# The spatial part of a gated mixing, made for the prompt's four tiles at once instead of two and two

## The chip, the cores and the metric

The kernel runs on one core of one Trainium2 chip. The metric is the device time of one execution in microseconds, the median of several runs. The core has a matmul engine (TensorE, "PE" in the profile; its weight loads are "PEld"), VectorE ("DVE"), ScalarE ("ACT"), GpSimdE ("POOL") and SyncE ("SP"), which issues the DMA transfers here.

## The reference

One step of a small streaming encoder with two layers, in fp32. A prompt of 512 frames (four tiles of 128 rows) and a sample batch of 8 x 16 frames (one tile) go through the same layers; the sample also reads caches of 1,024 frames. Each layer projects its input once and feeds three branches: a chunked gated mixing (A), a latent attention (B) and a stick-breaking attention (C). Their results are normalised, joined and projected, and a squared-ReLU MLP follows. The change is in branch A:

```python
def spatial_gate(u, v, w_s, b_s):
    b, s = u.shape[:2]
    c = min(s, GMLP_CHUNK)            # 128
    n_c = s // c
    idx = jnp.arange(c)
    w = jnp.where(chunk_visible(idx, idx)[None], w_s[:, :c, :c], 0)
    vc = v.reshape(b, n_c, c, G_A, DG_A)
    mixed = jnp.einsum('gij,bnjgd->bnigd', w, vc) + b_s[:, :c].T[None, None, :, :, None]
    return u * mixed.reshape(b, s, G_A, DG_A)
...
    u = jax.nn.gelu(a_u).reshape(b, s, G_A, DG_A)
    v = layer_norm(jax.nn.gelu(a_v).reshape(b, s, G_A, DG_A))
    y_a = spatial_gate(u, v, w_s, b_s).reshape(b, s, W_A)
...
    y = jnp.concatenate([rms_norm(y_a, g_a), rms_norm(y_b, g_b), rms_norm(y_c, g_c)], -1)
```

G_A is 4 groups of DG_A = 64 columns. A tile of 128 frames is one chunk, so each of the prompt's tiles is mixed by the same four 128 x 128 matrices.

## The kernel before, in words

Every fp32 matrix is split into a high and a low fp32r part (`split`: a ScalarE copy, then a VectorE difference), and a product is three matmuls (`mm3`, line 634). Two streams run beside each other: P (the prompt, and the projections of all five tiles) and S (the sample). A layer of P goes through the stages in, mix, mla, out and mlp; S goes through prep, smla, ssb, out and mlp, and begins its layer when the mix of that layer has been emitted.

The mix stage (`p_layer`) has two lanes: the prompt's stick-breaking attention (`lane_psb`) and `rest`. `rest` projects u and v, and then runs two lanes against each other (`lanes`, line 468; the one with the smaller matmul time divided by its weight goes next, if its operands are ready): `latents` with weight 1.0 and `gmlp` with weight 0.1 (`WM`, line 42). `latents` makes two projections, five tiles each: 384 columns (evicted by `rms_to` into `ev`, stored to `cqd`) and then 320 columns (`latent_to`: an rms norm and a rotation with two little tiles, stored to `ckd`). `gmlp` applies the gelu and calls `gm_weights` and `gm_group` for the sample tile, and then for the prompt's tiles 1 and 2, and 3 and 4. A group normalises `gv` (the v half), splits it into `gh`, multiplies by the split mixing weights `wsT`, adds the bias `bsc`, multiplies by `u` and normalises each tile into `xy` with `rms_to`.

The order of the work is made by a planner in the file. The emission is recorded as a list of operations; `ranks` (line 193) gives each a priority by its place in its stream, and `schedule` (line 209) plays all engines with a cost for each operation and lays down the order of every engine, DMA issues on SP included. Three things in it bind the order further. The slots of a ring (a tag with a number of buffers) are granted in the order of emission, and a tile's first instruction does not come before that of the tile emitted before it on the same ring (`grant`, line 271, and `begun`, line 250). The matmul results of the projections lie in `acc`, a ring of three PSUM banks; those of the mixing in `sC`, another ring of three. And the little sums and roots of `rms_to` (line 678) come from rings of three in stream P (line 541). A tile may begin only when all tiles of closed pools that lie under it in SBUF are done (`under`, line 241): pools grow from the left and from the right end, and `spans` gives their places.

At the mix stage the left stack holds, from byte 85,760: `xT` (32,768 bytes per partition), `xS` 8,192, `gcq` 1,536, `gckv` 1,024, `rope` 2,560, `ev` 4,096, `gvt` 5,120, `gmxa` 1,024, `gt` 2 x 2,048, `wsT` 4,096, `bsc` 32, `gh` 4,096, and two rope tiles of 256; it ends at 154,912. The sample's preparation (`s_prep`) lies on the right and reaches down to 155,360: `kd` from there, `qd` from 155,872, `wuT` from 159,968 to 168,160. `wuT` is made from a staging buffer of a ring of three, and the first cache loads of smla (`rawK`) lie on that ring's bytes.

```python
    def little(shape, dtype, tag):
        return sm.tile(shape, dtype, tag=tag + now["by"], name=tag, bufs=3 if now["by"] == "P" else 2)
    def rms_to(out, src, g, n):
        ss = little([128, 1], F32, "ss")
        act.activation(junk[now["by"]][:, :n], src, AF.Square, accum_out=ss)
        r = rstd_of(ss, 1.0 / n, 1)
        dve.scalar_tensor_tensor(out, src, r[:, 0:1], g, ALU.mult, ALU.mult)
```

Of the kernel before, what the change touches and what calls it, by code (L numbers as in the profile page):

```python
# [11 lines left out]
F32 = mybir.dt.float32  # L12
F32R = mybir.dt.float32r
BF16 = mybir.dt.bfloat16
AF = mybir.ActivationFunctionType
ALU = mybir.AluOpType
# [34 lines left out]
def r32(ap):  # L51
    return ap.bitcast(F32)


class Pace:
# [37 lines left out]
    def ready(self, *xs):  # L93
        return max([self.done.get(x.tensor.name, 0.0) for x in xs])
# [420 lines left out]
def hybrid_step(  # L515
# [11 lines left out]
    act, dve, pool, pe = (Timed(e, k, pace) for e, k in ((nc.scalar, "act"), (nc.vector, "dve"), (nc.gpsimd, "pool"), (nc.tensor, "pe")))  # L527
# [13 lines left out]
    def little(shape, dtype, tag):  # L541
        return sm.tile(shape, dtype, tag=tag + now["by"], name=tag, bufs=3 if now["by"] == "P" else 2)
# [38 lines left out]
    def bank(tag):  # L581
        return ps.tile([128, 512], F32, tag=tag, name=tag, bufs=BUFS[tag])

    def at(tag, *xs):

        return max([pace.bank((id(ps), tag), BUFS[tag])] + [x if isinstance(x, float) else ready(x) for x in xs])
# [43 lines left out]
    def split(hi, lo, src, lo_eng=None):  # L630
        act.copy(hi, src)
        sub(lo, src, hi, lo_eng)

    def mm3(out, ah, al, bh, bl, start, stop):
        pe.matmul(out, ah, bh, start=start, stop=False)
        pe.matmul(out, ah, bl, start=False, stop=False)
        pe.matmul(out, al, bh, start=False, stop=stop)
# [11 lines left out]
    def root(out, x, k):  # L649

        act.activation(out, x, AF.Ln, bias=eps, scale=k)
        act.activation(out, out, AF.Exp, scale=-0.5)
# [6 lines left out]
    def bcast(src, n, p=None, tag="gain", bufs=1):  # L659
        t = p.tile([128, n], F32, tag=tag, name=tag, bufs=bufs) if p else stage("S")[:, :n]  # L660
        ld.dma_start(t, src.partition_broadcast(128))
        return t
# [15 lines left out]
# [5 lines that stand above are left out]
# [72 lines left out]
    def gm_weights(l, pl, v, tag):  # L755


        wsn = pl.tile([128, 512], F32, tag="gt", name="gt", bufs=2).rearrange("p (g c) -> p g c", g=4)
        wsT = pl.tile([128, 2, 4, 128], F32R, tag="wsT", name="wsT")
        bsc = pl.tile([128, 4], F32, tag="bsc", name="bsc")  # L760
        ld.dma_start(wsn, (t_wss if v else t_ws)[l])
        ld.dma_start(bsc, (t_bss if v else t_bs)[l])
        if v == 1:
            split(wsT[:, 0], wsT[:, 1], wsn)
        else:
            pool.memset(r32(wsT[64:128, :, :, 0:64]), 0.0)
            split(wsT[0:64, 0], wsT[0:64, 1], wsn[0:64])
            split(wsT[64:128, 0, :, 64:128], wsT[64:128, 1, :, 64:128], wsn[64:128, :, 64:128])
        return wsT, bsc

    def gm_group(l, t0, nt, ws, gmx, gvt, pl, tag):

        wsT, bsc = ws
        ts = slice(t0, t0 + nt)
        gv = gvt[:, ts].rearrange("p t (g d) -> p t g d", d=64)
        u = xy[:, ts, 0:256].rearrange("p t (g d) -> p t g d", d=64)
        tmp = pl.tile([128, 512], F32, tag="gt", name="gt", bufs=2)[:, :nt * 256].rearrange("p (t g d) -> p t g d", g=4, d=64)

        def across(x):
            return x.unsqueeze(3).to_broadcast([128, nt, 4, 64])  # L780

        def stat():
            return little([128, 4, 4], F32, "gst")[:, :nt]

        mu = stat()
        dve.tensor_reduce(mu, gv, AX.X, ALU.add)
        dve.scalar_tensor_tensor(gv, across(mu), -1.0 / 64, gv, ALU.mult, ALU.add)
        act.activation(tmp, gv, AF.Square)
        var = stat()
        dve.tensor_reduce(var, tmp, AX.X, ALU.add)  # L790
        r = stat()
        root(r, var, 1.0 / 64)
        dve.tensor_tensor(gv, gv, across(r), ALU.mult)
        if t0 == 0:
            ld.dma_start(o_gv[l].rearrange("b s g d -> (b s) (g d)"), gvt[:, 0])
        gh = pl.tile([128, 2, 512], F32R, tag="gh", name="gh")[:, :, :nt * 256].rearrange("p a (g t d) -> p a g t d", g=4, d=64)
        split(gh[:, 0], gh[:, 1], gv.rearrange("p t g d -> p g t d"))
        ya = pl.tile([128, 512], F32, tag="gt", name="gt", bufs=2)[:, :nt * 256].rearrange("p (t g d) -> p t g d", g=4, d=64)
        yield at(tag, gh, wsT)
        pm = bank(tag)[:, :nt * 256].rearrange("p (g c) -> p g c", g=4)  # L800
        for g in range(4):
            mm3(pm[:, g], wsT[:, 0, g], wsT[:, 1, g], gh[:, 0, g].rearrange("p t d -> p (t d)"),
                gh[:, 1, g].rearrange("p t d -> p (t d)"), True, True)
        dve.tensor_tensor(ya.rearrange("p t g d -> p g t d"), pm.rearrange("p g (t d) -> p g t d", d=64),
                          bsc.unsqueeze(2).unsqueeze(3).to_broadcast([128, 4, nt, 64]), ALU.add)
        dve.tensor_tensor(ya, ya, u, ALU.mult)
        for t in range(nt):
            rms_to(xy[:, t0 + t, 0:256], ya[:, t].rearrange("p g d -> p (g d)"), gmx, 256)
# [4 lines left out]
    def p_layer(l):  # L813
# [105 lines left out]
        def gmlp():  # L919
            gmx = bcast(g_mix[l, 0:256], 256, den, "gmxa")  # L920
            k0 = len(pace.plan.ops)
            act.activation(xy[:, :, 0:256], xy[:, :, 0:256], AF.Gelu_apprx_tanh)
            act.activation(gvt, gvt, AF.Gelu_apprx_tanh)
            act.preload_act_table_set("natural_log_exp_and_others")
            pace.plan.glue(k0)
            for v, groups in ((1, ((0, 1),)), (0, ((1, 2), (3, 2)))):
                ws = gm_weights(l, den, v, GT)
                for t0, nt in groups:
                    yield from gm_group(l, t0, nt, ws, gmx, gvt, den, GT)

        def rest():
            for t, pa in project(O_U, 512):
                if pa is None:
                    yield t
                else:
                    act.copy(xy[:, t, 0:256], pa[:, 0:256])
                    act.copy(gvt[:, t], pa[:, 256:512])
            yield from lanes(pace, (latents(), WM[1]), (gmlp(), WM[2]))
# [984 lines left out]
```

## Time and profile before

| | us |
|---|---|
| median of 3 runs (1724.64 to 1727.94) | 1726.88 |
| the profiled execution's own time | 1729.99 |
| its span | 1728.2 |
| PE busy | 1661.9 |
| VectorE busy | 1204.0 |
| ScalarE busy | 1022.4 |

The profile is of one execution. "Busy" is time in which an instruction of the engine is open. The granted clock is TensorE's, as a share of 2.4 GHz; it has two levels, 1.0 and 0.5, and a mean between them is a stretch with both. Nearly every instruction carries line 433, that of the recording helper, so rows are told apart by the names of their tiles, written out<-in. `acc`, `sC` and `x` are PSUM banks, `gh`, `gt`, `gvt` and `wsT` are the mixing's tiles, `ev` is an evicted latent, `junkP` takes the squares of a norm.

### The profile page before, as it was taken

To read this page: it belongs to the slowest core of one execution; us is meant where nothing else is said; L and a number is where in the kernel's file an instruction comes from. 1 tells how busy PE (TensorE), PEld (TensorE's weight loads), DVE (VectorE), ACT (ScalarE), POOL (GpSimd) and SP (SyncE) were. 2 spreads that over 40 slices of the span, in tenths; PEclk is the share of its full clock that TensorE was granted. 3 is DMA by queue.
4 is the path that set the end of the run, shared out by engine and by line. 5 is a ranking of instruction groups with operands and counts; after the bars stand their busy time and mean duration, and the time that the engine had idled before them with its cause. 6 is when DMAs were issued, how large, how long until landed. Compare 5 with 4: busy or idle time off the path is not lost.

```text
span 1728.2 us, 24196 instructions
## 1 busy us (share of the span) xinstructions
PE 1661.9 (96%) x8684; PEld 1397.6 (81%) x8684; DVE 1204.0 (70%) x1702; ACT 1022.4 (59%) x1969; POOL 246.6 (14%) x192
## 2 busy tenths in 40 slices
PE   8998999899999999999999989999999999999998
PEld 6898888787888778888778989787778777788886
DVE  3487676857887777666735867768478877766756
ACT  4585784646765656463335858856468656564631
POOL 0000444552000000000000004465410000000000
PEclk9998999899999999999999989999999999999999
DMA  7334565456545677674452355654555546776732
GB/s 250 104 96 157 166 197 197 147 156 197 177 156 150 222 263 251 184 255 126 139 176 83 94 172 183 206 176 159 165 182 174 165 131 249 256 246 192 243 124 85
DMA packets 145017, 304.65 MB, mean 176 GB/s; under 512 B 32512, under 2 KB 44928, under 8 KB 144896
## 3 DMA queue, kind: packets, MB, share of 16 engines
q1 hardware_dynamic: 144896, 303.10, 54.4%
q8 instruction: 68, 1.11, 0.3%
q14 instruction: 53, 0.43, 0.1%
HBM read 285.75 MB, written 17.30 MB: 175 GB/s over the span
## 4 chain that ended last, share of the span: by engine, by line
PE 74%; DVE 8%; DMA 7%; ACT 6%; issue 2%; POOL 1%; SPq 0%; ACTq 0%; POOLq 0%; DVEq 0%
PE acc L433 54%; PE sC L433 11%; PE x L433 10%; DVE xy L433 2%; DMA rawK<-in_t_sbk_dram 1%; DVE w L433 1%; DMA rawV<-in_t_ckvv_dram 1%; DMA krs<-in_t_kr_dram 1%; ACT cT L433 1%; ACT w L433 1%; DMA rawV<-in_t_sbv_dram 1%; POOL cN L433 1%; DMA rawS<-in_w_down_dram 1%; ACT cN L433 1%; DMA rawS<-in_w_up_dram 1%
## 5 line engine op out<-in xcount | busy, mean ns | idle before, releaser
L433 PE MATMUL acc<-yT,wx 128*128 128x512 f32 (+1 forms) x1632 | 395.9, 387 | 2.5 <-DVE wx L433 2.5
L433 PE MATMUL acc<-w,hT 128*128 128x512 f32 x1536 | 396.5, 397 | 0.0
L433 PEld LDWEIGHTS acc<-yT,wx 128*128 128x128 f32 x1632 | 291.3, 192 | 60.5 <-DVE wx L433 3.2
L433 PEld LDWEIGHTS acc<-w,hT 128*128 128x128 f32 x1536 | 281.0, 188 | 62.1 <-DVE xy L433 0.4
L433 DVE TENSOR_TENSOR wS<-rawS,wS 128x1024 fp32r<-128x1024 f32 x144 | 175.4, 1223 | 75.9 <-ACT wS L433 75.2
L433 ACT CAST wS<-rawS 128x1024 fp32r<-128x1024 f32 x144 | 150.7, 1050 | 111.6 <-PE x L433 54.8
L433 DVE TENSOR_TENSOR w<-rawP,w 128x1024 fp32r<-128x1024 f32 (+3 forms) x120 | 143.8, 1202 | 96.7 <-ACT w L433 96.2
L433 PE MATMUL acc<-w,xT 128*128 128x512 f32 (+3 forms) x960 | 195.4, 359 | 8.1 <-DVE ev L433 5.7
L433 PEld LDWEIGHTS acc<-w,xT 128*128 128x128 f32 x960 | 163.2, 198 | 27.0 <-DVE ev L433 6.2
L433 ACT CAST w<-rawP 128x1024 fp32r<-128x1024 f32 (+3 forms) x120 | 121.8, 1016 | 73.2 <-DMA rawP<-in_w_down_dram 36.3
L433 DVE TENSOR_TENSOR xy<-xy,acc 128x512 f32<-128x512 f32 x128 | 87.0, 683 | 46.9 <-PE acc L433 46.7
L433 ACT CAST cN<-rawV 128x512 fp32r<-128x512 f32 x128 | 78.1, 619 | 60.7 <-DMA rawV<-in_t_ckvv_dram 20.6
L433 POOL TENSOR_TENSOR cT<-rawK,cT 128x512 fp32r<-128x512 f32 x64 | 92.4, 1450 | 119.4 <-ACT cT L433 101.0
L433 ACT CAST cT<-rawK 128x512 fp32r<-128x512 f32 x128 | 79.3, 621 | 48.1 <-PE sC L433 21.3
L433 DVE TENSOR_TENSOR wx<-rawP,wx 128x1024 fp32r<-128x1024 f32 x68 | 88.3, 1300 | 23.0 <-ACT wx L433 22.3
L433 POOL TENSOR_TENSOR cN<-rawV,cN 128x512 fp32r<-128x512 f32 x64 | 91.2, 1433 | 85.1 <-ACT cN L433 67.1
L433 PE MATMUL sC<-wS,x1TS 128*128 128x512 f32 x384 | 99.4, 394 | 0.4 <-DVE wS L433 0.3
L433 PE MATMUL x<-wS,htS 128*128 128x512 f32 x384 | 98.5, 393 | 1.2 <-ACT htS L433 1.2
L433 PE MATMUL x<-cN,pTs 128*128 128x256 f32 x512 | 91.2, 288 | 4.0 <-ACT cN L433 2.3
L433 PEld LDWEIGHTS x<-cN,pTs 128*128 128x128 f32 x512 | 77.9, 188 | 20.9 <-ACT cN L433 6.4
L433 PEld LDWEIGHTS x<-wS,htS 128*128 128x128 f32 x384 | 71.7, 188 | 18.5 <-ACT htS L433 2.1
L433 PEld LDWEIGHTS sC<-wS,x1TS 128*128 128x128 f32 x384 | 71.6, 188 | 18.0 <-DVE wS L433 2.1
(278 smaller groups left out, 2667.2 us busy)
## 6 DMA issues: line engine op xcount, KB each, us to landing
rawP<-in_t_wup_dram SPq DMA_DIRECT2D x64, 512.0 KB, 4.0
rawP<-in_w_down_dram SPq DMA_DIRECT2D x64, 512.0 KB, 3.9
rawS<-in_w_up_dram SPq DMA_DIRECT2D x64, 512.0 KB, 4.6
rawS<-in_w_down_dram SPq DMA_DIRECT2D x64, 512.0 KB, 4.2
rawK<-in_t_ckv_dram SPq DMA_DIRECT2D x64, 256.0 KB, 3.1
rawV<-in_t_ckvv_dram SPq DMA_DIRECT2D x64, 256.0 KB, 3.1
rawK<-in_t_sbk_dram SPq DMA_DIRECT2D x64, 256.0 KB, 2.9
rawV<-in_t_sbv_dram SPq DMA_DIRECT2D x64, 256.0 KB, 3.1
```

What stands on the lines that cost most here:

```text
L433: r = f(out, *a, **k)
```

## The change

The prompt's four tiles form one group. `gt` (two slots) and `gh` are twice as wide, and the matmuls of a group of four tiles fill two PSUM banks, two mixing groups each, one after the other with a bias addition behind each. The sample's group keeps its one bank.

```diff
     def gm_weights(l, pl, v, tag):
-        wsn = pl.tile([128, 512], F32, tag="gt", name="gt", bufs=2).rearrange("p (g c) -> p g c", g=4)
+        wsn = pl.tile([128, 1024], F32, tag="gt", name="gt", bufs=2)[:, :512].rearrange("p (g c) -> p g c", g=4)
...
     def gm_group(l, t0, nt, ws, gmx, gvt, pl, tag):
-        tmp = pl.tile([128, 512], F32, tag="gt", name="gt", bufs=2)[:, :nt * 256].rearrange("p (t g d) -> p t g d", g=4, d=64)
+        tmp = pl.tile([128, 1024], F32, tag="gt", name="gt", bufs=2)[:, :nt * 256].rearrange("p (t g d) -> p t g d", g=4, d=64)
...
-        gh = pl.tile([128, 2, 512], F32R, tag="gh", name="gh")[:, :, :nt * 256].rearrange("p a (g t d) -> p a g t d", g=4, d=64)
+        gh = pl.tile([128, 2, 1024], F32R, tag="gh", name="gh")[:, :, :nt * 256].rearrange("p a (g t d) -> p a g t d", g=4, d=64)
         split(gh[:, 0], gh[:, 1], gv.rearrange("p t g d -> p g t d"))
-        ya = pl.tile([128, 512], F32, tag="gt", name="gt", bufs=2)[:, :nt * 256].rearrange("p (t g d) -> p t g d", g=4, d=64)
-        yield at(tag, gh, wsT)
-        pm = bank(tag)[:, :nt * 256].rearrange("p (g c) -> p g c", g=4)
-        for g in range(4):
-            mm3(pm[:, g], wsT[:, 0, g], wsT[:, 1, g], gh[:, 0, g].rearrange("p t d -> p (t d)"),
-                gh[:, 1, g].rearrange("p t d -> p (t d)"), True, True)
-        dve.tensor_tensor(ya.rearrange("p t g d -> p g t d"), pm.rearrange("p g (t d) -> p g t d", d=64),
-                          bsc.unsqueeze(2).unsqueeze(3).to_broadcast([128, 4, nt, 64]), ALU.add)
+        ya = pl.tile([128, 1024], F32, tag="gt", name="gt", bufs=2)[:, :nt * 256].rearrange("p (t g d) -> p t g d", g=4, d=64)
+        ng = 4 if nt < 4 else 2
+        for g0 in range(0, 4, ng):
+            yield at(tag, gh, wsT)
+            pm = bank(tag)[:, :ng * nt * 64].rearrange("p (g c) -> p g c", g=ng)
+            for g in range(g0, g0 + ng):
+                mm3(pm[:, g - g0], wsT[:, 0, g], wsT[:, 1, g], gh[:, 0, g].rearrange("p t d -> p (t d)"),
+                    gh[:, 1, g].rearrange("p t d -> p (t d)"), True, True)
+            dve.tensor_tensor(ya[:, :, g0:g0 + ng].rearrange("p t g d -> p g t d"), pm.rearrange("p g (t d) -> p g t d", d=64),
+                              bsc[:, g0:g0 + ng].unsqueeze(2).unsqueeze(3).to_broadcast([128, ng, nt, 64]), ALU.add)
         dve.tensor_tensor(ya, ya, u, ALU.mult)
...
         def gmlp():
-            for v, groups in ((1, ((0, 1),)), (0, ((1, 2), (3, 2)))):
+            for v, groups in ((1, ((0, 1),)), (0, ((1, 4),))):
```

## Rows read from the trace of the kernel before

**Rows 1.** The page's parts 1 and 4: busy time, and the last chain by engine.
```profile
PE 1661.9 (96%) x8684; PEld 1397.6 (81%) x8684; DVE 1204.0 (70%) x1702; ACT 1022.4 (59%) x1969; POOL 246.6 (14%) x192
...
PE 74%; DVE 8%; DMA 7%; ACT 6%; issue 2%; POOL 1%; SPq 0%; ACTq 0%; POOLq 0%; DVEq 0%
```

**Rows 2.** Windows of 24 us: length, busy PE, PEld, DVE, ACT, POOL; clock, DMA.
```profile
120.00:144.00 24.00, 20.61 (x133) 19.55 (x133) 20.61 (x34) 18.52 (x56) 0.52 (x1) 0.93 0.61 194
144.00:168.00 24.00, 22.71 (x146) 22.12 (x146) 14.64 (x40) 10.79 (x33) 1.02 (x2) 0.85 0.46 141
...
984.00:1008.00 24.00, 20.91 (x123) 20.29 (x122) 19.89 (x35) 16.66 (x51) 0.00 (x0) 0.85 0.65 198
```

**Rows 3.** PE's waits over the span: releaser, us in total, times, longest.
```profile
PE acc L433 <- DVE ev L433: 5.7, 2, 2.8
```

**Rows 4.** Timeline of PE, 126 to 163 us: start, length, instruction, count, idle before.
```profile
129.42 0.31 PE L433 MATMUL acc<-w,xS 128*128 128x320 f32 x1
...
133.35 1.34 PE L433 MATMUL sC<-gh,wsT 128*128 128x128 f32 x11
...
136.05 2.50 PE L433 MATMUL acc<-w,xT 128*128 128x320 f32 x16
141.40 1.17 PE L433 MATMUL acc<-w,xT 128*128 128x320 f32 x3 [2.84 <-DVE ev L433]
...
145.64 2.44 PE L433 MATMUL sC<-gh,wsT 128*128 128x128 f32 x11
...
158.14 0.82 PE L433 MATMUL acc<-identr,rawP 128*128 128x128 f32 x6
```

**Rows 5.** Timeline of ScalarE and VectorE around the stall, 136 to 143 us.
```profile
136.65 0.42 ACT L433 ACTIVATE junkP<-gt 128x256 bf16<-128x256 f32 x1
...
138.42 0.47 ACT L433 ACTIVATE junkP<-acc 128x384 bf16<-128x384 f32 x1
...
140.73 0.61 DVE L433 SCALAR_TENSOR_TENSOR ev<-acc,rs,gcq 128x384 f32<-128x384 f32 x1
...
141.25 1.05 ACT L433 CAST wuT<-rawS 128x1024 fp32r<-128x1024 f32 x1 [1.11 <-DMA rawS<-in_t_wukT_dram]
```

**Rows 6.** Windows of 2 us around the stall, columns as in rows 2.
```profile
138.00:140.00 2.00, 0.56 (x4) 0.29 (x3) 2.00 (x5) 2.00 (x13) 0.00 (x0) 1.00 0.94 316
...
148.00:150.00 2.00, 2.00 (x9) 2.00 (x9) 1.78 (x5) 0.43 (x2) 0.00 (x0) 0.50 0.00 1
...
152.00:154.00 2.00, 2.00 (x16) 2.00 (x15) 1.35 (x5) 0.86 (x4) 0.45 (x2) 1.00 0.40 122
```

**Rows 7.** Groups of whole-span instructions by form: count, busy us, mean ns, idle before.
```profile
L433 DVE TENSOR_TENSOR wS<-rawS,wS 128x1024 fp32r<-128x1024 f32 x144 | 175.4, 1223 | 75.9 <-ACT wS L433 75.2
L433 ACT CAST wS<-rawS 128x1024 fp32r<-128x1024 f32 x144 | 150.7, 1050 | 111.6 <-PE x L433 54.8 <-PE sC L433 37.2 <-DMA rawS<-in_w_up_dram 9.4
...
L433 DVE TENSOR_TENSOR gt<-gt,xy x6: 425/680/683, 122.2 to 1008.5; 128x512 f32<-128x512 f32 x4, 128x256 f32<-128x256 f32 x2
L433 ACT ACTIVATE junkP<-gt x10: 398/417/418, 122.7 to 1010.0; 128x256 bf16<-128x256 f32 x10
```

**Rows 8.** Timeline, matmuls of 256 columns in the next stage.
```profile
164.44 1.60 PE L433 MATMUL acc<-ckT,w 128*128 128x256 f32 x12
```

**Rows 9.** Tiles, 100 to 240 us: count, ns min/median/max, first and last start.
```profile
L433 ACT CAST wuT<-rawS x1: 1047/1047/1047, 141.2 to 141.2; 128x1024 fp32r<-128x1024 f32 x1
L433 PE MATMUL sC<-qT,wuT x24: 220/274/280, 192.0 to 195.3; 128*128 128x128 f32 x24
...
L433 DVE TENSOR_TENSOR ev<-rp,rp x5: 217/224/227, 145.2 to 162.1; 128x64 f32<-128x64 f32 x5
...
L449 SPq DMA_DIRECT2D rawK<-in_t_ckv_dram x14: 327/328/3673, 143.6 to 238.9; - x14
L433 ACT CAST cT<-rawK x12: 616/620/651, 184.9 to 236.9; 128x512 fp32r<-128x512 f32 x12
```

**Rows 10.** Timeline of PE in layer 1, the first reload of the latents.
```profile
1024.38 0.71 PE L433 MATMUL acc<-identr,rawP 128*128 128x128 f32 x4 [2.02 <-DMA rawP<-ckd]
```

## The prediction

> **What bounds the kernel now.** I read the page's shares first: the matmul engine is busy 96% of the span and carries 74% of the chain that ended last [rows 1]. So a microsecond counts only where TensorE stands still or runs slowly. The second view is the windows table: idle PE time and a low granted clock come in a few places, and two of them are the end of the mixing stage, once per layer. From 120 to 144 us PE is busy 20.61 of 24 us at a mean clock of 0.93, and the next 24 us run at 0.85; layer 1 repeats it at 984 to 1008 us (20.91 us, 0.85) [rows 2]. That is where the changed lines run. The third view, PE's waits, names the releaser: `acc` waiting for `ev` twice, 2.8 us each, one per layer [rows 3].
>
> The fourth view, the timeline, shows why. The five latent tiles of 320 columns (I call them K1 to K5, 24 matmuls each) start at 129.42. PE stops after the second and waits 2.84 us until 141.40 [rows 4]. `acc` has three banks, so K3 needs the bank of the last 384-column tile (Q5), freed by its eviction `ev` at 140.73. Q5's squares ran only at 138.42, right behind the squares of the gated mixing's own norms, `junkP<-gt`, at 136.65 [rows 5]. Q5's matmuls stand before K1's in PE's order, so they were over by 129.6, and this is order and not data: `rms_to` takes its little sum from a ring of three, and the planner grants such a ring in the order of emission. The two norms of the first prompt pair are emitted after the fourth 384-column tile and before Q5, so Q5's eviction has to follow the pair's whole chain. After the stall the clock is at its lower level (0.5 of 2.4 GHz, that is 1.2): the means 0.93 and 0.85 of 24 us make 3.4 + 7.2, about 10.6 us at half speed [rows 2]; it is back at 1.00 by 152 us [rows 6]. In it the second pair's eleven matmuls take 2.44 us, against 1.34 us for the first pair's [rows 4].
>
> **The change, part by part (one layer; times of layer 0).**
>
> Matmuls. 24 of 128 columns become 12 of 256. At full clock 11 of 128 columns take 1.34 us, so 24 take 2.9; twelve of 256 columns take 1.60 us [rows 4, 8]. Saved: 1.3 us, all on PE, more if the second pair's run at half speed goes with it. The Trainium skill, TensorE: Matmul & The Clock Gate, section "Back-to-back issue gap", speaks against this: it gives an isolated matmul its columns over 2.4 GHz plus about 2.5 ns, 56 ns for 128 and 109 ns for 256, so that 24 and 12 would cost the same 1.3 us and nothing were saved here. The row's 122 ns for 128 columns does not agree with 56.
>
> VectorE and ScalarE. Of each pair's chain, VectorE has two reductions, three products or differences on `gv`, the bias and the product with `u`: 14 instructions of 0.68 us, 9.5 us for both pairs. They become six of 1,024 elements, for which I take the 1.22 us of a 128x1024 difference, and two bias additions of 0.68: 8.7 us [rows 7]. ScalarE saves one root and the fixed part of a square and a cast, under 1 us. The four norms stay. What is widened early (mean and subtraction near 108 us) costs VectorE about 1.1 us more there; the cover is PE's queue of latent matmuls, and without it the stick-breaking lane ends up to 1.1 us later: bound 0 to 1.1, taken as 0.
>
> Order of the ring, the largest term. The new group has a share of `12 x 0.111 + 6 x 0.119 = 2.05` us of matmul after its first half; at weight 0.1 that is 20.5 against 16.8 for four 384-column tiles and 21.0 for five. So the second half and the four norms are emitted after Q5 and before K1. Q5's eviction no longer follows the group, and K3 starts without the 2.84 us wait. The new wait is one tile later: K1's eviction now stands behind four norms on the ring, and K4 needs its bank. PE's arrival there: 129.4, three tiles of 24 x 0.157 us (16 take 2.50 [rows 4]) = 11.3, the group's 1.6 and 0.3 of an existing gap: 142.6. K1's eviction: VectorE is continuously busy until Q5's `ev` ends at 141.3. Up to K1's `ev` that queue loses the second pair's four instructions (2.7 us) and gains four widenings of 0.54, a second bias, two more norms' products (0.9) and the eviction itself (0.5), net +1.5: 142.8. ScalarE's side gains two norms (2.2 us), K1's own (1.1) and the widenings (0.9), loses 1.1 of the second pair's chain, and is late by some 3 us: 143.9. The later decides: a stall of 1.3 us, bounds 0 and 4 (4 if ScalarE waits once more on a weight load, as it does at 141.25 [rows 5]).
>
> End of the latents. Five tiles at 3.76 us, 1.6, 0.3 and 1.3 after 129.4 give 151.4, if the clock stays up; today the next stage's first transposes run at 158.14 [rows 4]. Gain 6.7 us, of which 1.3 are the matmuls, 1.5 the stall, and the rest the half-speed stretch. If a stall still brings the clock down for as long as today, 5 us of it are lost again: gain 1.7.
>
> What is late next. The next stage reads the latents back from DRAM; in layer 1 PE already waits 2.02 us for such a load [rows 10], and that load hangs on K3's eviction, which now follows four norms. Bound 0 to 4 us, taken as 1.7, near that row.
>
> A moved region. The two `gt` slots and `gh` grow by 8,192 bytes together. From the sizes in the code, the left stack's top rises from 154,912 to 163,104, past the sample preparation's bottom at 155,360. So `wuT` (159,968 to 168,160) now lies on `gh` and on the latents' little rope tiles, and its cast waits for the last of these: today at 141.2, then not before the last rope, today 162.1 [rows 9]. Its staging buffer is held longer, and with it the first `rawK` loads, issued at 143.6 on SP's queue; SP's later loads keep their planned order. Cover: `wuT` is first read at 192.0 and `rawK` at 184.9 [rows 9], 20 us of slack. But the two `wuT` instructions, 1.05 on ScalarE and 1.22 on VectorE [rows 7], move from the old stall into the start of the next stage, where PE waits on those engines: bound 0 to 2.3, taken as 1.0.
>
> Sum. 6.7 less 1.7 less 1.0 is 4.0 us per layer; both layers show the same stall [rows 3], so 8.0. The profiled execution took 1729.99 us (span 1728.2); less 8.0 it is 1722.0. It stood 3.1 above the median 1726.88, so the forecast is 1718.9, rounded 1719.
>
> **The rivals.** About 0.2% (3.5 us: 1723.4 and 1730.3) is what a measurement of this kernel can tell from no change.
>
> Larger gain: nothing is late next, 6.7 us per layer: 1713.5. For it: 20 us of slack for `wuT`; against: the 2.02 us wait [rows 10].
>
> Equal: K1's eviction comes as late as Q5's did, the stall is about as long and the clock falls again. Then 1.7 per layer remains, less 1.0 for the moved instructions: 1.4 us in all, 1725.5.
>
> Slower: the four norms in a row keep K1's bank until about 146.5. The stall is then 4 us, the half-speed stretch is repeated whole (5 us), so the latents end at 129.4 + 18.8 + 1.9 + 4 + 5 = 159.1 instead of 158.1; with 1.0 for `wuT` and 1.0 more for the reloaded latents that is 3 us per layer: 1733. It decides from a stall of about 3 us at K4. For it: ScalarE's waits on loads in this stretch [rows 5]; against: VectorE's sum above.
>
> Columns bound: a matmul of 256 columns costs twice one of 128. Then 12 take 2.9 us, the 1.3 us per layer is not saved, and the time is 1721.5. Against it: 1.60 us for twelve [rows 8]. The Trainium skill's figures on the issue gap, above, lead to this case.
>
> The change doesn't do what it says: the group's second half is emitted later than worked out, after K1 or K2. Then Q5 and K1 are both free of the norms and the gain is the larger one; I count it there.
>
> **How the numbers follow.** Forecast 0.46, larger gain 0.13, columns bound 0.03, equal 0.19, slower 0.19. The first three are faster, but 0.02 of the forecast's spread falls within 0.2%: faster 0.60, within 0.2% 0.21, slower 0.19. The range must reach the equal case and take in the larger gain with its bounds (two layers at 6.7, and up to 2 us each if the second pair's slow run counts fully): 1710 to 1731; left out are most of the slower case and the far tail below, 0.2 together.
>
> **What would show it.** Right: in the changed trace no wait of `acc` for the 384-column `ev` near 138 us; Q5's squares before the first `junkP<-gt`; a shorter wait one tile later; a clock of 1.00 around 145 us; `wuT` cast after the last rope. Wrong: a wait at K4 of 3 us or more with the clock at half behind it; twelve group matmuls in over 2 us at full clock; PE idle longer after the latents than today.

## The result, and the profile after

The changed kernel took 1717.92 us (median of 4 runs, 1716.36 to 1719.57) beside 1726.76 us of the kernel before on the same chip: a ratio of 0.9948, 95% interval 0.9933 to 0.9963, or 8.8 us. The forecast was 1719.0. The profiled execution took 1716.36 us and its span is 1714.6, 13.6 us below that of before; 4.7 of these lie in the choice of execution, since the one profiled before stood 3.1 us above its median and this one stands 1.6 below.

Parts 1 and 4 of the page of the changed kernel, which answer [rows 1]:

```profile
PE 1653.5 (96%) x8660; PEld 1386.7 (81%) x8660; DVE 1211.3 (71%) x1690; ACT 1020.9 (60%) x1961; POOL 247.8 (14%) x192
...
PE 61%; DVE 6%; DMA 6%; ACT 5%; issue 1%; POOL 1%; SPq 0%; ACTq 0%; DVEq 0%; POOLq 0%
```

PE has the 24 instructions fewer that the diff promises. The windows, against [rows 2] (columns as there), and PE's waits, against [rows 3]:

```profile
120.00:144.00 24.00, 21.72 (x147) 20.78 (x146) 20.49 (x32) 18.30 (x58) 0.52 (x1) 1.00 0.63 189
144.00:168.00 24.00, 22.60 (x158) 21.87 (x157) 16.83 (x45) 13.68 (x39) 5.30 (x5) 0.93 0.54 175
...
984.00:1008.00 24.00, 22.17 (x147) 20.82 (x146) 19.51 (x48) 15.29 (x56) 0.43 (x1) 1.00 0.62 194
```

```profile
PE acc L433 <- DMA rawP<-ckd: 4.0, 2, 3.3
...
PE acc L433 <- DVE ev L433: 0.5, 2, 0.2
```

The wait of 5.7 us for `ev` is down to 0.5. In layer 0 the clock that was 0.93 and 0.85 is 1.00 and 0.93. What took the place of the stall is in PE's timeline (start, length, instruction, count, idle before), against [rows 4]:

```profile
128.17 0.36 PE L433 MATMUL acc<-w,xS 128*128 128x320 f32 x1
...
132.86 0.40 PE L433 MATMUL sC<-gh,wsT 128*128 128x256 f32 x2
...
134.71 1.33 PE L433 MATMUL sC<-gh,wsT 128*128 128x256 f32 x10
...
136.32 5.45 PE L433 MATMUL acc<-w,xT 128*128 128x320 f32 x36
141.60 0.49 PE L433 MATMUL sC<-identr,cq 128*128 128x128 f32 x3
143.50 0.62 PE L433 MATMUL sC<-wq,cqT 128*128 128x384 f32 x2 [1.40 <-ACT cqT L433]
144.35 2.17 PE L433 MATMUL sC<-wq,cqT 128*128 128x384 f32 x7 [0.24 <-DVE cqT L433]
146.32 8.11 PE L433 MATMUL acc<-w,xT 128*128 128x320 f32 x48
154.26 0.82 PE L433 MATMUL acc<-identr,rawP 128*128 128x128 f32 x6
```

K1 to K3 run to 141.8 with no wait for Q5's bank. K4 starts only at 146.32, and in between PE works for the **sample's preparation**: transposes of `cq`, then products with `wq` (`s_prep`). In the kernel before these began at 158.8, behind the latents. ScalarE and VectorE in the same stretch, against [rows 5]:

```profile
127.95 0.47 ACT L433 ACTIVATE junkP<-acc 128x384 bf16<-128x384 f32 x1
...
130.81 0.61 DVE L433 SCALAR_TENSOR_TENSOR ev<-acc,rs,gcq 128x384 f32<-128x384 f32 x1
139.60 0.42 ACT L433 ACTIVATE junkP<-gt 128x256 bf16<-128x256 f32 x1 [0.68 <-DVE gt L433]
...
142.53 0.36 ACT L433 ACTIVATE junkP<-acc 128x256 bf16<-128x256 f32 x1
...
144.21 0.47 DVE L433 SCALAR_TENSOR_TENSOR ev<-acc,rs,gckv 128x256 f32<-128x256 f32 x1
...
144.61 0.34 DVE L433 TENSOR_TENSOR rp<-acc,rope 128x64 f32<-128x64 f32 x2
...
159.64 1.06 ACT L433 CAST wuT<-rawS 128x1024 fp32r<-128x1024 f32 x1
```

Q5's squares now run 11.7 us ahead of the group's first `junkP<-gt`; K1's eviction is behind all four norms; `wuT` is cast behind the last rope.

**Where the time went.** The same instructions in all the traces, in us. "Latents" is from K1's first matmul to the first matmul behind K5, in layer 0; the end of mla0 is the first product of the stage out, `acc<-w,yT`; the other shifts are against the kernel before; "wuT" is the start of the sample's products with `wuT` in layer 0; ratios, as recorded, are with their 95% intervals; they are not the quotients of the medians.

| kernel | latents | first product with ckT | wuT at | end of mla0 (first product with yT) | K1 of layer 1 | ratio of the times |
|---|---|---|---|---|---|---|
| before | 28.7 | 0 | 192.0 | 0 | 0 | 1 |
| changed | 26.1 | -2.9 | 167.3 | -9.8 | -9.7 | 0.9948 (0.9933, 0.9963) |
| e5 changed again | 26.0 | -3.1 | 167.2 | -9.5 | -8.8 | 0.9952 (0.9933, 0.9970) |
| e1 | 21.1 | -1.9 | 188.7 | -0.7 | +2.2 | 0.9988 (0.9970, 1.0007) |
| e2 | 30.6 | +1.1 | 193.0 | +2.3 | +0.8 | 1.0002 (0.9983, 1.0022) |
| e3 | 27.1 | -1.5 | 190.9 | +1.6 | +1.1 | 1.0032 (1.0016, 1.0048) |
| e4 | 26.6 | +4.3 | 168.9 | -3.6 | -0.5 | 1.0062 (1.0039, 1.0085) |
| e6 | 24.0 | -5.8 | 174.9 | -13.7 | -10.4 | 0.9925 (0.9904, 0.9945) |
| e7 | 21.1 | -2.0 | 188.7 | -2.5 | -3.1 | 0.9980 (0.9966, 0.9993) |
| e8 | 25.3 | -2.4 | 193.1 | -4.5 | +2.2 | 1.0027 (1.0010, 1.0044) |
| e9 | 19.5 | -7.8 | 175.3 | -15.7 | -9.5 | 0.9924 (0.9905, 0.9943) |
| e10 | 27.1 | -1.9 | 168.3 | -8.9 | -8.5 | 0.9968 (0.9950, 0.9987) |
| e11 | 24.0 | -5.2 | 175.5 | -13.2 | -12.0 | 0.9924 (0.9907, 0.9941) |
| e12 | 24.0 | -5.8 | 174.7 | -14.1 | -12.5 | 0.9922 (0.9904, 0.9941) |

Each row is one execution. Some lie far from the median of their kernel (e6 6.4 us above it, e9 6.2 and e10 5.8 below), but the two kernels that were profiled twice (changed and e5, e6 and e12) agree within 0.4 us up to the end of mla0, and within 2.2 us at K1 of layer 1.

In the changed kernel 1.25 us of the shift is there before K1; kernels whose code up to there is that of before also start K1 up to 1.0 us earlier (e6, e12), so it is put down to the execution. Layer 0 then gains 2.6 us by the end of the latents, 1.7 by the first product with `ckT` and 8.6 by the end of mla0, and keeps it. Layer 1 gains 4.7, 3.2 and 1.6 at the same places and 3.6 by TensorE's last matmul. So less than a third of layer 0's gain is in the stage where the code was changed.

### The profile page after: what moved, and what is told of

It reads as the page before. It is cut to its first block, busy times and chain, and to the rows that moved or that the text cites. A ratio compares the mean times of both kernels' runs of the same rounds, so it can differ in the third digit from the quotient of the medians.

```text
span 1714.6 us, 24115 instructions
## 1 busy us (share of the span) xinstructions
PE 1653.5 (96%) x8660; PEld 1386.7 (81%) x8660; DVE 1211.3 (71%) x1690; ACT 1020.9 (60%) x1961; POOL 247.8 (14%) x192
## 4 chain that ended last, share of the span: by engine, by line
PE 61%; DVE 6%; DMA 6%; ACT 5%; issue 1%; POOL 1%; SPq 0%; ACTq 0%; DVEq 0%; POOLq 0%
PE acc L433 43%; PE sC L433 9%; PE x L433 9%; DMA rawK<-in_t_sbk_dram 1%; DVE xy L433 1%; DMA rawV<-in_t_ckvv_dram 1%; DMA rawV<-in_t_sbv_dram 1%; POOL cN L433 1%; DMA rawS<-in_w_up_dram 1%; ACT cT L433 1%; ACT w L433 1%; ACT cN L433 1%; DMA rawP<-in_w_down_dram 1%; DVE w L433 1%; DVE a L433 1%
## 5 line engine op out<-in xcount | busy, mean ns | idle before, releaser
L433 PE MATMUL acc<-w,xT 128*128 128x512 f32 (+3 forms) x960 | 187.6, 350 | 2.8 <-ACT w L433 1.1
L433 PEld LDWEIGHTS acc<-w,xT 128*128 128x128 f32 x960 | 157.9, 191 | 21.6 <-ACT w L433 1.5
L433 PEld LDWEIGHTS x<-cN,pTs 128*128 128x128 f32 x512 | 78.7, 188 | 18.2 <-ACT cN L433 4.3
L433 PEld LDWEIGHTS sC<-wS,x1TS 128*128 128x128 f32 x384 | 71.6, 188 | 18.2 <-DVE wS L433 2.1
```

What stands on the lines that cost most here:

```text
L433: r = f(out, *a, **k)
```

## The experiments

The runs stand in three groups, each on one chip with the kernel before beside it; its medians there were 1729.95 (e1 to e4), 1728.29 (e5 to e8) and 1731.10 (e9 to e12), so ratios are compared, not times.

**e1 and e2: what ties Q5 to the pair's norms.** In the kernel before, the mixing's norms get little sums of their own (e2), or those and another scratch tile for the squares, `junk["S"]` (e1, whose diff is shown; e2 has `scratch` nowhere):

```
-    def little(shape, dtype, tag):
-        return sm.tile(shape, dtype, tag=tag + now["by"], name=tag, bufs=3 if now["by"] == "P" else 2)
+    def little(shape, dtype, tag, ring=""):
+        return sm.tile(shape, dtype, tag=tag + now["by"] + ring, name=tag, bufs=3 if now["by"] == "P" else 2)
...
-    def rms_to(out, src, g, n):
-        ss = little([128, 1], F32, "ss")
-        act.activation(junk[now["by"]][:, :n], src, AF.Square, accum_out=ss)
-        r = rstd_of(ss, 1.0 / n, 1)
+    def rms_to(out, src, g, n, ring="", scratch=None):
+        ss = little([128, 1], F32, "ss", ring)
+        act.activation((scratch or junk[now["by"]])[:, :n], src, AF.Square, accum_out=ss)
+        r = rstd_of(ss, 1.0 / n, 1, ring)
...
-            rms_to(xy[:, t0 + t, 0:256], ya[:, t].rearrange("p g d -> p (g d)"), gmx, 256)
+            rms_to(xy[:, t0 + t, 0:256], ya[:, t].rearrange("p g d -> p (g d)"), gmx, 256, "G", junk["S"])
```

> The kernel before (two pairs), but the gated mixing's own norms take their little sums and roots from a ring of their own and put their squares into the other stream's scratch tile, so that the eviction of the fifth 384-column latent no longer follows the first pair's norms. Instructions, tiles of the mixing and matmuls are those of before. Theory (the order couples Q5's eviction to the mixing): no 2.8 us wait of acc on the 384-column ev in either layer, the clock at 1.00 behind it, and a time between 1716 and 1722. Rival (fewer and wider instructions, larger matmuls): nothing of that is changed here, so 1725 to 1728.

> The kernel before, with only the ring of the little sums and roots made separate for the mixing's norms; their squares still go into the common scratch tile. If the ring alone holds Q5's eviction back, as the prediction had it: 1717 to 1722, the wait gone. If the scratch tile, which each norm's squares overwrite in the order of emission, holds it as well: Q5's squares stay behind the pair's, both waits of 2.8 us stay, 1725 to 1729.

Measured: e1 1727.04 us beside 1729.95, e2 1728.92. PE's waits of e2 have the line of [rows 3] to the digit:

```profile
PE acc L433 <- DVE ev L433: 5.7, 2, 2.8
```

Freeing the ring alone does nothing: every norm of the prompt also writes its squares into one tile, `junkP`, and these writes keep their order of emission. The scratch tile alone was not freed, so whether the ring binds too is not shown. With both freed (e1) there is no wait for `ev` any more and the latents are 7.6 us shorter, and the time is still within 0.2% of before, which misses the 1716 to 1722 us expected if Q5's order is the whole gain. PE's waits of e1 from 144 to 168 us, and windows of 24 us:

```profile
PE acc L433 <- DMA rawP<-ckd: 2.9, 1, 2.9
PE acc L433 <- DVE rp L433: 1.6, 1, 1.6
```

```profile
120.00:144.00 24.00, 23.74 (x166) 23.13 (x166) 21.15 (x39) 18.27 (x59) 0.52 (x1) 1.00 0.61 195
144.00:168.00 24.00, 19.20 (x134) 18.11 (x134) 15.07 (x37) 11.91 (x32) 1.01 (x2) 0.86 0.54 158
```

The stall has moved behind the latents: TensorE arrives earlier and stands still for the last rope and the reloaded latents, 4.8 us idle in that window and the clock down to 0.86. Removing the stall alone is not the gain.

**e3: only the wider tiles.** The kernel before with `gt` and `gh` as wide as in the changed one, still two pairs (each of the three `gt` tiles, and `gh`):

```
-        tmp = pl.tile([128, 512], F32, tag="gt", name="gt", bufs=2)[:, :nt * 256].rearrange("p (t g d) -> p t g d", g=4, d=64)
+        tmp = pl.tile([128, 1024], F32, tag="gt", name="gt", bufs=2)[:, :nt * 256].rearrange("p (t g d) -> p t g d", g=4, d=64)
...
-        gh = pl.tile([128, 2, 512], F32R, tag="gh", name="gh")[:, :, :nt * 256].rearrange("p a (g t d) -> p a g t d", g=4, d=64)
+        gh = pl.tile([128, 2, 1024], F32R, tag="gh", name="gh")[:, :, :nt * 256].rearrange("p a (g t d) -> p a g t d", g=4, d=64)
```

> The kernel before, with gt and gh as wide as after the change and nothing else: the left stack's top rises by 8,192 bytes and wuT has to wait for the last rope tile. Order theory: the stall at K3 stays at 2 to 3 us, the wuT cast leaves it; 1725 to 1730. Rival (moving the wuT instructions out of the stall is the gain): 1718 to 1722. Cost theory of the moved region (1.0 us per layer in the next stage): 1728 to 1730.

Measured: 1734.88 beside 1729.95 us, slower by 0.3% and beyond every range that was expected. `wuT` moves onto the widened region, its cast behind the last rope and so into the start of the next stage. PE in layer 1, then VectorE:

```profile
1028.39 0.34 PE L433 MATMUL acc<-identr,kd 128*128 128x128 f32 x1 [2.96 <-DVE cqT L433]
```

```profile
1026.35 0.29 DVE L433 TENSOR_TENSOR rp<-sC,rope 128x128 f32<-128x128 f32 x1 [5.66 <-ACT qn L433]
1026.56 1.22 DVE L433 TENSOR_TENSOR wuT<-rawS,wuT 128x1024 fp32r<-128x1024 f32 x1
1027.69 1.01 DVE L433 TENSOR_TENSOR cqT<-acc,cqT 128x384 fp32r<-128x384 f32 x2
```

TensorE waits 2.96 us for `cqT`, which in VectorE's order stands behind `wuT` and behind a rope product of the sample that waits 5.66 us for `qn`; in the kernel before `cqT` was done at 1023.3, ahead of both. The moved region costs through the order more than through its 2.3 us of work. The prediction took 1.0, bound 2.3.

**e4: the merged group's norms ahead of Q5.** The changed kernel, emitting the merged group before Q5:

```
-WM = (1.0, 1.0, 0.1)
+WM = (1.0, 1.0, 0.125)
...
-            yield at(tag, gh, wsT)
+            yield 0.0 if nt == 4 else at(tag, gh, wsT)
```

> The changed kernel with the same single group of four tiles, but emitted so that all its matmuls and its four norms come before Q5's eviction (the lane's weight 0.125 instead of 0.1, and the group not held back until gh is ready). Order theory: acc waits again for the 384-column ev, now behind four norms, for 3 us or more; the clock falls; 1724 to 1733. Rival (the wide group as such is the gain): 1716 to 1720, as after the change.

Measured: 1738.36 beside 1729.95 us, 0.6% slower than before, beyond the range expected. Layer 1:

```profile
1004.55 8.82 PE L433 MATMUL acc<-w,xT 128*128 128x320 f32 x48 [4.22 <-DVE ev L433]
...
1027.57 0.34 PE L433 MATMUL acc<-identr,kd 128*128 128x128 f32 x1 [2.96 <-DVE cqT L433]
```

The wait for Q5's `ev` is back, as order theory had it; the wait for `cqT` behind the latents is e3's, so part of the loss is the moved region's. Merging by itself gains nothing: with its norms emitted early the changed kernel is slower than before. In layer 0 the sample's preparation filled the same place (`wuT` at 168.9), and that layer is 3.6 us ahead at the end of mla0 although its first product with `ckT` is 4.3 us late. That made the sample's start the suspect.

**e5 to e8: the sample's start.** The sample's first tile of `sC` is granted behind the last tile of the mixing, in order of emission; in the kernel before that is the second pair's, whose `gh` is ready only after the stall. e6 is the kernel before with that pair on the ring `x` (the first edit below); e7 is e1 with the same edit; e8 is the changed kernel with a load that holds the preparation back (the second):

```
-                    yield from gm_group(l, t0, nt, ws, gmx, gvt, den, GT)
+                    yield from gm_group(l, t0, nt, ws, gmx, gvt, den, "x" if t0 == 3 else GT)
...
+        ld.dma_start(cq0[:, :320], ckd[:, 4])
         ld.dma_start(cq0, cqd[:, 0])
```

> The changed kernel itself, as the reference for the three kernels beside it. If this chip agrees with the first comparison, 7 to 11 us less than the kernel before.

> The kernel before; only the bank of the second prompt pair comes from the ring x of two instead of the ring sC of three, so that the sample's preparation, which takes the next sC banks, need not be granted behind it. Start theory (the sample's preparation begins in the latents, fills TensorE's waits there and in the next stage, and this is what lasts): the first transposes of cq run before 145 us in layer 0 instead of at 158.8, the product with wuT before 175 instead of at 192.0, and the time is 5 to 11 us below the kernel before, though the 2.8 us eviction stall or part of it is still there. Stall theory (the time comes from the eviction stall and the clock behind it alone): within 2 us of the kernel before.

> The kernel before with the mixing's norms on a ring and a scratch tile of their own (as in e1_both_free) and the second pair's bank from the ring x. Start theory: the latents end some 6 us earlier as in e1_both_free and the sample's preparation runs before 150 us, so that less is given back behind the latents: 6 to 13 us below the kernel before. Stall theory: as e1_both_free, 1 to 3 us below the kernel before.

> The changed kernel; one load more per layer holds the sample's preparation until the fifth 320-column tile is written to DRAM (the same bytes are loaded over it afterwards, and nothing else is changed). Start theory: the cq transposes run after 155 us as before the change, and most of the gain goes: 3 us below to 2 us above the kernel before. Stall theory: the latents still have no eviction stall before the fourth tile, and the time stays 6 to 9 us below the kernel before.

Measured, beside 1728.29: e5 1722.74, e6 1715.93, e7 1726.24, e8 1734.51 us. PE of e6 in layer 0, and the stall of layer 1:

```profile
135.03 2.51 PE L433 MATMUL acc<-w,xT 128*128 128x320 f32 x16
137.38 0.49 PE L433 MATMUL sC<-identr,cq 128*128 128x128 f32 x3
138.49 0.62 PE L433 MATMUL sC<-wq,cqT 128*128 128x384 f32 x2 [0.62 <-ACT cqT L433]
139.84 0.79 PE L433 MATMUL sC<-wq,cqT 128*128 128x384 f32 x3 [0.73 <-DVE cqT L433]
...
991.35 1.17 PE L433 MATMUL acc<-w,xT 128*128 128x320 f32 x3 [2.84 <-DVE ev L433]
```

One line, and none of the merging, gives 0.75% (e12 again: 0.78%). Q5's eviction is as late as before, but in layer 0 TensorE works through that time; from 120 to 168 us the clock stays at 1.00. In layer 1 (the last row) the preparation came only at 1004.8, the stall stands in full, and e6 gains nothing from K1 to the end of that layer. The load of `cq`, which the preparation transposes, is part of the reason. SP of e6 in layer 0, then PE and SP in layer 1:

```profile
125.77 0.59 SPq L449 DMA_DIRECT2D cq<-cqd  x1
...
975.85 3.69 PE L433 MATMUL acc<-w,xS 128*128 128x384 f32 x20
...
994.17 0.38 SPq L449 DMA_DIRECT2D cq<-cqd  x1
```

In layer 0 it is issued some 11 us ahead of the stall's place. In layer 1 the sample's tile (`xS`) is the last of the 384-column tiles, Q5 itself, so its load comes behind the late eviction and the stall, which a free bank could not fill; the changed kernel, with Q5 freed, issues it at 985.8 and transposes at 993.4. Stall theory's figure, within 2 us, is missed by 10; start theory's 5 to 11 us are exceeded by 1 to 2.

e8 goes the other way: without the early preparation the changed kernel is 0.3% slower than before, some 5 us, where start theory allowed 2. PE of e8:

```profile
145.99 8.82 PE L433 MATMUL acc<-w,xT 128*128 128x320 f32 x48 [3.08 <-DVE rp L433]
```

This is K4's wait with nothing to fill it: 3.08 us. The experiment is not pure: the held load stands in SP's queue, the preparation starts at 171.3, later than in the kernel before, and in layer 1 PE also waits 4.02 us for a reload of `cqd` behind it. In layer 0 TensorE waits 1.0 us for the held load itself and for no reload behind it; there the 9.8 us at the end of mla0 fall to 4.5, and the layer ends 2.2 us late.

e7 missed what start theory expected (6 to 13 us below; measured 2.0 us, ratio 0.9980). With no stall PE ran the latents through to 149.8, and the preparation began at 150.1 although its bank was free: a freed bank helped only where there was a wait to fill.

**e9: the changed kernel with Q5 and K1 both freed.** e1's diff, applied to the changed kernel.

> The changed kernel with the mixing's norms on a ring and a scratch tile of their own, so that neither Q5 nor K1 waits for the four norms. Stall theory: the wait before K4 goes, and the time is lower still than the changed kernel's, 9 to 14 us below the kernel before. Start theory: without that wait nothing lets the sample's preparation in before the latents end (as in e7_both_and_x), it begins near 149 us instead of 141.6, TensorE stands still behind the latents instead, and most of the gain goes: 1 to 5 us below the kernel before.

Measured: 1716.08 beside 1731.10 us, 0.76% below before. Here start theory alone falls: its 1 to 5 us are missed by at least 8, while stall theory's 9 to 14 hold by the ratio. As start theory expected, hardly any of the preparation ran in the latents (two transposes at 140.65, the first product with `wq` at 150.26), and the gain is there all the same. PE behind the latents, and the windows of 48 us of the two layers:

```profile
148.07 0.49 PE L433 MATMUL acc<-identr,rawP 128*128 128x128 f32 x3
...
149.98 0.52 PE L433 MATMUL acc<-identr,rawP 128*128 128x128 f32 x3 [1.31 <-DVE rp L433]
...
153.44 0.63 PE L433 MATMUL acc<-identr,rawP 128*128 128x128 f32 x4 [0.75 <-DMA rawP<-ckd]
```

```profile
120.00:168.00 48.00, 45.15 (x326) 43.20 (x325) 39.64 (x82) 34.26 (x98) 3.07 (x5) 1.00 0.65 198
...
984.00:1032.00 48.00, 44.15 (x337) 41.98 (x337) 38.35 (x86) 31.89 (x93) 7.15 (x8) 1.00 0.65 204
```

The reloaded latents are awaited for 0.75 us instead of e1's 2.9, and the clock stays up in both layers. Two things differ from e7, and no run parts them: VectorE has the merged, shorter chain, and `wuT` (2.3 us on ScalarE and VectorE) is cast behind the reload, at 153.6, instead of among the latents' evictions, at 144.6.

**e10: the matmuls alone.** The changed kernel with 24 matmuls of 128 columns and the mixing lane's weight 0.13, with which the order of emission stays:

```
+                for h in range(0, nt, 2):
+                    c = slice(h * 64, min(h + 2, nt) * 64)
+                    mm3(pm[:, g - g0, c], wsT[:, 0, g], wsT[:, 1, g], gh[:, 0, g].rearrange("p t d -> p (t d)")[:, c],
+                        gh[:, 1, g].rearrange("p t d -> p (t d)")[:, c], True, True)
```

> The changed kernel with the merged group's products issued as 24 matmuls of 128 columns again instead of 12 of 256 (the order of emission is the same). The matmuls cost 2.9 us instead of 1.6 per layer. If the saved 1.3 us per layer counted, the gain shrinks by 2.6 us to about 6 us below the kernel before; if TensorE only reaches its wait before K4 that much later, it stays 7 to 11 us below.

Measured: 1725.21 beside 1731.10 us, ratio 0.9968 against 0.9948 and 0.9952. The intervals overlap, so the time does not decide; its median, 5.9 us below before, lies nearer to the case in which the 1.3 us per layer count. The trace gives the price:

```profile
135.31 2.57 PE L433 MATMUL sC<-gh,wsT 128*128 128x128 f32 x22
```

**e11 and e12: a better version.** e12 is e6 again; e11 is e6 in layer 0 and the merged group in layer 1, with the tiles' widths `1024 if l else 512`:

```
-            for v, groups in ((1, ((0, 1),)), (0, ((1, 4),))):
+            for v, groups in ((1, ((0, 1),)), (0, ((1, 4),) if l else ((1, 2), (3, 2)))):
...
-                    yield from gm_group(l, t0, nt, ws, gmx, gvt, den, GT)
+                    yield from gm_group(l, t0, nt, ws, gmx, gvt, den, "x" if t0 == 3 else GT)
```

> Layer 0 as e6_pair2_on_x (two pairs, the second one's bank from the ring x, narrow tiles), layer 1 as the changed kernel (four tiles at once). If what each layer gained in the traces stays with that layer, layer 0 gives 11 us and layer 1 some 3 us: 12 to 16 us below the kernel before, better than either. If layer 1's gain needs what layer 0 did, 9 to 12 us.

> The kernel of e6_pair2_on_x again, beside e11_x_then_merged on one chip: 9 to 16 us below the kernel before if its first interval holds.

Measured, beside 1731.10: e11 1716.76, e12 1717.06 us. From its K1 to its end layer 1 of e11 gains 2.4 us; that of e6 and e12 loses 3.2 and 1.8. The ratio of e11 is inside the 12 to 16 us that were expected, but it is not better than e12, as it should then have been. e9, e11 and e12 are below the changed kernel's ratio by some 0.25%, with intervals that just overlap its own; among the three nothing can be told.

## Why the prediction was right, step by step

The time came out 1.1 us below the forecast. That it came so close is luck in part: some of its steps failed, and their errors cancelled.

- **Matmuls.** Right. Ten of 256 columns take 1.33 us and twenty-two of 128 take 2.57 (e10), the prices that [rows 4, 8] had given, so the "columns bound" rival is out. The 56 ns for 128 columns that the prediction weighed, from the Trainium skill, TensorE: Matmul & The Clock Gate, section "Back-to-back issue gap", are given there for an isolated matmul, and the section itself says that they fall short of a stream. The stream here shows 117 ns.
- **The order of Q5.** The effect was right (Q5's squares at 127.95, `ev` wait gone), the cause half: the prediction named the ring of three little sums; e2 shows that freeing the ring alone changes nothing, e1 that the shared scratch tile has to go too.
- **The wait at K4.** Mis-sized. TensorE came at 141.8 (142.6 forecast) and K1's `ev` at 144.21 (143.9), but the bank is read once more, by the rope products until 144.95. With nothing in between the wait is 3.08 us (e8), not 1.3; it was inside the bounds, and at the point of 3 us from which the prediction let the slower rival decide. e4 and e8 come out slower, at +0.6% and +0.3%, but not by that rival's sum, which had the latents end later than before: theirs are 2.1 and 3.4 us shorter in layer 0, and they lose behind them.
- **What fills that wait.** Missing from the prediction, and by e6 and e8 the largest part of the gain, though e8 is not pure and e9 gains as much in another way: the sample's preparation. The prediction counted `sC` only as the mixing's bank and did not ask who is granted the next one.
- **The clock.** Forecast at 1.00 around 145 us; the waits of 1.40 and 0.24 us for `cqT` leave TensorE busy 1.36 of 3 us from 142 to 145, and it runs at half speed behind them, for about 3.4 us where the prediction had counted 10.6 before, as the windows of 2 us show. Half speed behind K4 was part of a sign of being wrong that the prediction named:

```profile
144.00:146.00 2.00, 1.76 (x7) 1.65 (x7) 1.47 (x6) 1.22 (x8) 0.00 (x0) 0.72 0.35 131
146.00:148.00 2.00, 2.00 (x9) 2.00 (x9) 1.04 (x6) 0.37 (x1) 0.00 (x0) 0.50 0.49 164
```

- **End of the latents.** Gain 2.6 us in layer 0 and 4.7 in layer 1 instead of 6.7: K4's longer wait, the half-speed stretch, and the sample's matmuls that now lie inside it. e1 shows that 7.6 is there to be had, and that it is worth next to nothing by itself.
- **What is late next.** In layer 0 the sign failed. Of the 2.6 us, 0.9 was lost up to the first product with `ckT`, but by the end of mla0 the gain was 8.6, since the sample's stream ran some 23 us ahead and gave TensorE work in the next stage's gaps: from 168 to 240 us it idles 2.7 us instead of 5.6. In layer 1 3.1 of 4.7 us were given back, as forecast (2.7); there the reloaded latents are awaited for 3.3 us instead of 2.0, another of those signs. The difference between the layers shows in windows from the first product with `ckT` to the first with `yT`, before (layers 0 and 1), then after:

```profile
164.44:255.23 90.79, 83.19 (x621) 75.92 (x619) 65.15 (x140) 72.77 (x184) 39.58 (x30) 1.00 0.54 167
1029.00:1111.69 82.69, 78.47 (x601) 72.99 (x600) 63.82 (x135) 69.57 (x178) 33.52 (x28) 1.00 0.54 160
...
161.50:245.42 83.92, 80.12 (x607) 73.57 (x605) 67.79 (x136) 72.88 (x183) 41.05 (x31) 1.00 0.63 188
1016.10:1100.32 84.22, 79.41 (x600) 72.70 (x599) 65.64 (x132) 70.82 (x180) 36.71 (x29) 1.00 0.55 167
```

In layer 0 TensorE's idle time falls from 7.6 to 3.8 us and 14 matmuls, of the sample's, have moved out of the stretch. In layer 1 it was idle for only 4.2 us before the change, so there was little to fill; it is 4.8 after.
- **The moved region.** Seen as forecast (`wuT` cast at 159.64). It cost nothing visible here; in e3 it cost a wait of 2.96 us.
- **The sum.** Forecast 4.0 and 4.0; the trace shows 8.5 and 3.6, besides the 1.25 ahead of K1 and 0.2 behind TensorE's last matmul. Less the 4.7 us that lie in the choice of the two executions this is 8.9, beside the 8.8 of the medians, so how much of each layer's gain is the execution's cannot be told.

Open: why the kernel before has more idle time in mla0 than in mla1, so that a lead of the sample (23.4 and 18.2 us behind K1) pays in the first alone; what in e9 makes up for the late preparation; and why its 15.7 us at the end of mla0 are 9.5 by layer 1.

## What to carry to other kernels

In this kernel, removing a wait from the busiest engine moved it to the next place where a slower engine has not caught up; it paid where the wait's place was filled, or where the next place was ready too. So ask not only what a shared ring or scratch tile makes late, but which other stream is granted its next buffer behind it: one bank taken from another ring was worth at least as much here as the whole merging. And when a release is timed, follow the bank to its last reader, not to the eviction that carries its name.

## What was not expected of the hardware

The clock does not follow the idle time simply. In the changed kernel 1.64 us idle within 142 to 145 us are followed by half speed until 148; in e9 TensorE is idle for 2.6 us within 148 to 154, in pieces of up to 1.31 us, and the granted clock stays at 1.00. The windows of the changed kernel and of e9:

```profile
142.00:145.00 3.00, 1.36 (x6) 0.95 (x6) 3.00 (x10) 3.00 (x17) 0.00 (x0) 0.98 0.72 275
```

```profile
148.00:154.00 6.00, 3.42 (x23) 2.60 (x21) 4.66 (x14) 3.44 (x12) 1.01 (x2) 1.00 0.62 200
```

No run here was made to tell why.
